# Eight plain gate tiles in the first feed-forward, later sums of the norm, and the low parts of the embedding's gate weights by adding transfers

## The chip, the cores and the metric

The kernel runs on one core of one Trainium2 chip. The metric is device time in microseconds (us) of one execution of the whole program, lower is better; times of several executions are given as their median.

## The reference, cut to what matters

Two layers on 512 tokens of 1024 features, in f32. Each layer adds to `x`: half a gated feed-forward, a token mixer, another half feed-forward, and a gated per-layer embedding; every one of these begins with a norm of `x`.

```
def swiglu_ffn(h, w_gu, w_down):
    a, b = jnp.split(h @ w_gu, 2, axis=-1)
    return (jax.nn.silu(a) * b) @ w_down
...
    for i in range(DEPTH):
        x = x + 0.5 * swiglu_ffn(rms_norm(x, ffn1_norm[i]), ffn1_w_gu[i], ffn1_w_down[i])
        ...
        x = x + 0.5 * swiglu_ffn(rms_norm(x, ffn2_norm[i]), ffn2_w_gu[i], ffn2_w_down[i])
        gate = jax.nn.sigmoid(rms_norm(x, ple_norm[i]) @ ple_w_gate[i])
        x = x + gate * (p[i] @ ple_w_proj[i])
    return rms_norm(x, final_norm)
```

The feed-forward's inner width is 1408, which is 11 tiles of 128 columns; a "gate tile" is one such tile of the gate half `a` and of the up half `b` together.

## The kernel before, in words

**Layout and precision.** `x` is held as eight tiles `x[m]` of 128 features by 512 tokens. Every product is three matmuls in a reduced f32 format (fp32r): each operand is split into a high part (a rounded copy) and a low part (the value minus the rounded copy), and high·high, high·low and low·high are summed in PSUM. For a weight tile, `w_cut` (L259) does this: ACT copies the high part into `wh` (L260), DVE subtracts it from the loaded tile `wr` to give `wl` (L261). A tile of weights is loaded by one SP transfer (`w_load`), from a ring of `WR` = 8 buffers (5 of them ahead for ungrouped tiles), and `wh` and `wl` have `WS` = 4 buffers each. `weight` (L321) hands out the weights in the order of a `plan` made up front, and loads and splits as far ahead as buffers allow. `source` says where in DRAM a planned tile lies.

**The norm.** Its sums of squares are taken by eight narrow matmuls into a bank `pss` (`columns`, L587); `inv_rms` scales them on DVE (`v`, L600) and takes the power on POOL (`rc`, L602). Until `rc` is there, products run on values without it, and the factor is put on behind them.

**The feed-forward, the seven-product way.** `ffn7` (L686) treats a range of gate and up columns (a "group") as a 2 by 2 block matrix and uses seven block products in the place of eight, in the manner of Strassen: B11, B21, T1, T2, B22, T3, T4. Each product is 24 matmuls, so a group of 384 columns (three gate tiles) has 168 matmuls of 384 columns. The weights of T1 to T4 are differences of loaded blocks, made by DVE (`w_term`, L289), and then split as above; for the first group of a feed-forward, T1's are pinned to the order of the program (`w_pin`). The activations of the products come from `Norm7.steps` (L523): per pair of tiles of `x`, sums and differences of half tiles on DVE (L532, L558 to L560) with their high parts on ACT (L534, L562, L563) and low parts on DVE (L538, L567, L569). The results have tokens on partitions and are turned by PE transposes, four to a gate tile, eight together behind the next group's first product (`turn`, L708).

**The first feed-forward of layer 0** has no earlier work to hide its start, so its first `KC` = 5 gate tiles go the plain way (`start` L640, then `gates` L664): per tile two banks A and B of 24 matmuls of 512 columns, scaled by the norm's row R and gated on DVE and ACT (`gated`, L790 to L794, and L401 for the low part). At the end of tile f = 3, `gates` runs `norm.steps` of all eight tiles of `x`. The other six tiles are two groups of 384 columns (`groups_of`, L1657). Late constants, which POOL loads (`late_constants`, L368, transfers L376) and the rotary tables, follow as `during` of the same function.

**Sums in `ffn7`.** In the other three feed-forwards the sums are not yet there when the first group begins, and `norm.sums()` stands behind the product T1 (L744), ahead of the copies of T1's banks (`copies`, L719) and of product T2.

**The embedding's gate of layer 0** (`ple`, L805): eight weight tiles `pg` of 512 KB, each with 24 matmuls into a bank G, and two tiles `pp` for the embedding's own projection J. Behind each G a chain updates a tile of `x`: DVE times R, ACT sigmoid, DVE times J, DVE add, then `steps` of the next norm. From the second tile on DVE is kept in program order here (`Queue`, whose instructions the profile shows as L123). Layer 1's feed-forward, the seven-product way, follows directly.

**Order.** Apart from what is pinned, a planner orders each engine's queue when the kernel is built, by its own cost model; buffers come from pools, 64 slabs of 128 by 512 for the activations.

Of the kernel before, what the change touches and what calls it, by code (L numbers as in the profile page):

```python
# [13 lines left out]
AF = mybir.ActivationFunctionType  # L14
ALU = mybir.AluOpType
# [3 lines left out]
P = 128  # L19
# [3 lines left out]
KD = D // P  # L23
FF = 1408
# [84 lines left out]
def tile_kernel(ctx: ExitStack, tc: tile.TileContext, a: dict, out: bass.AP):  # L109
    nc = tc.nc  # L110
    act, dve, pe, pool = nc.scalar, nc.vector, nc.tensor, nc.gpsimd
# [40 lines left out]
    plan = []  # L152

    def ffn_plan(w, l):
        if (w, l) == (1, 0):
            for f in range(KC):
                plan.append(("gu", f))
                plan.append(("gu", KC + f))
        for g in range(len(groups_of(w, l))):
# [63 lines left out]
    raw, ready = {}, {}  # L223
    at = [0, 0, 0]
    FIRST = 2
# [3 lines left out]
    loads, needs, done = [], [], []  # L229
    base, grouped = {}, set()  # L230
    for key in plan:
# [7 lines left out]
        if g not in base:  # L239
# [3 lines left out]
            n = 2 * groups_of(w_, l_)[g_][1]  # L243
            src = a[f"sg{w_}{l_}{g_}"]
# [18 lines left out]
    def w_tiles():  # L263
        hi = wp.tile([P, WCOLS], F32R, tag="wh", name=nm("wh"), bufs=WS)
        lo = wp.tile([P, WCOLS], F32R, tag="wl", name=nm("wl"), bufs=WS)
        return hi, lo

    def kept(i):

        k = plan[i]  # L270
        return k[0] == "pgl" or (k[0] in ("eo", "oo") and k[1] < OPEN)

    def wc(w, o):
        return w[o // S][:, o % S : o % S + P] if isinstance(w, list) else w[:, o : o + P]

    def w_pin(key):


        if key[3] == 0 and key[4] == "T1":
            return tc.keep_in_program_order  # L280
        return lambda ins: ins
# [18 lines left out]
    def w_split():  # L300
        i = at[1]
        if plan[i][0] == "sg":
            t, n = w_term(plan[i])
            ready[i] = w_tiles()
            w_cut(t, n, *ready[i], slice(0, n), w_pin(plan[i]))
            at[1] += 1
            return
        t, n = raw.pop(needs[i] - 1)
        if kept(i):
            parts = [[sl("kh", F32R) for _ in range(2)], [sl("kl", F32R) for _ in range(2)]]  # L310
            for c in range(2):
                src = t[:, c * S : c * S + S]
                act.copy(parts[0][c], src)
                dve.tensor_tensor(parts[1][c], src, f32(parts[0][c]), op=ALU.subtract)
            ready[i] = parts
        else:
            ready[i] = w_tiles()
            w_cut(t, n, *ready[i], slice(0, n))
        at[1] += 1
# [320 lines left out]
    def start(norm):  # L640

        table("silu_and_others")
        warm = bank("warm")
        for _ in range(WARM):
            pe.matmul(warm, ones_r, ones_r[:, 0:1].to_broadcast([P, S]), start=True, stop=True)
# [18 lines left out]
    def gates(norm, begun):  # L664

        g, wait = [], [begun]
        for f in range(1, KC):
            w = weight("gu", f)
            if f == 1:
                norm.squares()  # L670
            A = proj(w, 0, KD, norm.parts, "A")
            if f == 2:
                norm.sums()
            B = proj(weight("gu", KC + f), 0, KD, norm.parts, "B")
            if f == 2:
                norm.row()
            wait.append((A, B))
            while norm.R is not None and wait:
                gated(*wait.pop(0), norm.R, g)
            if f == 3:  # L680
                for m in range(KD):
                    for _ in norm.steps(m, False):
                        pass
        return g

    def ffn7(w, l, norm, nxt, g=None, during=None, after=None):  # L686


        rc = norm.rc if g else None
        groups = groups_of(w, l)  # L690
        g, turning = g or [], []

        def product(accs, gi, term, first, last):
            n = groups[gi][1]
            units = [weight("sg", w, l, gi, term, u) for u in range(2)]
            for t in range(2):
                for j in range(KD // 2):
                    (h, lw), c = norm.side(term, j)
                    cs = slice(c + t * P, c + t * P + P)
                    wh, wl = units[j // 2]  # L700
                    ws = slice((j % 2) * n, (j % 2) * n + n)
                    o = accs[t][:, :n]
                    begin, end = first and j == 0, last and j == KD // 2 - 1
                    pe.matmul(o, h[:, cs], wh[:, ws], start=begin, stop=False, skip_group_check=True)  # L704
                    pe.matmul(o, h[:, cs], wl[:, ws], start=False, stop=False, skip_group_check=True)  # L705
                    pe.matmul(o, lw[:, cs], wh[:, ws], start=False, stop=end, skip_group_check=True)  # L706

        def turn(count):  # L708
            for _ in range(min(count, len(turning))):
                tiles, i = turning.pop(0)  # L710
                pt = bank("gT")
                for b in range(NB):
                    pe.transpose(pt[:, b * P : b * P + P], tiles[b][:, i * P : i * P + P], ident)
                g.append(split(pt, "g"))

        def copies(accs, n):
            out_ = [sl("r") for _ in range(2)]
            for t in range(2):
                act.copy(out_[t][:, :n], accs[t][:, :n])  # L719
            return out_  # L720

        def add(tiles, accs, n):
            for t in range(2):
                dve.tensor_tensor(tiles[t][:, :n], accs[t][:, :n], tiles[t][:, :n], op=ALU.add)

        def close(c, o, srcs, b0, n):
            for t in range(2):
                r = rc[:, b0 + t : b0 + t + 1]
                act.activation(c[t][:, :n], srcs[t][:, :n], AF.Silu, scale=r)
                dve.scalar_tensor_tensor(o[t][:, :n], o[t][:, :n], r, c[t][:, :n], op0=ALU.mult, op1=ALU.mult)  # L730

        for gi, (_, n) in enumerate(groups):
            two = lambda name: [bank(name) for _ in range(2)]
            al = two("al")
            product(al, gi, "B11", True, False)
            c11 = copies(al, n)
            turn(2)
            be = two("be")
            product(be, gi, "B21", True, True)
            add(c11, be, n)  # L740
            turn(2)
            ga = two("ga")
            product(ga, gi, "T1", True, False)
            if rc is None:  # L744
                rc = norm.sums()
            c22 = copies(ga, n)
            product(al, gi, "T2", False, False)
            c12 = copies(al, n)
            product(ga, gi, "B22", False, True)
            add(c12, ga, n)  # L750
            close(c11, c12, c11, 0, n)
            product(al, gi, "T3", False, False)
            add(c22, al, n)
            product(al, gi, "T4", False, True)
            s2 = [sl("r") for _ in range(2)]
            close(s2, c22, al, 2, n)
            turning.extend(([*c12, *c22], i) for i in range(n // P))
        if during:
            during()

        def part(acc, wt, k0, k1, c0):
            wh, wl = wt
            for kk in range(k0, k1):
                o = slice((kk - c0) * P, (kk - c0) * P + P)
                mm3(acc, wh[:, o], wl[:, o], g[kk][0], g[kk][1], kk == 0, kk == KF - 1)

        cut = DN[0] // P
        early = KF - groups[-1][1] // P
        accs = [bank("dn"), None]
        part(accs[0], weight("dn", w, l, 0, 0), 0, cut, 0)  # L770
        w01 = weight("dn", w, l, 0, 1)
        part(accs[0], w01, cut, early, cut)
        turn(2)
        accs[1] = bank("dn")
        part(accs[1], weight("dn", w, l, 1, 0), 0, cut, 0)
        turn(2)
        part(accs[0], w01, early, KF, cut)
        for m in range(KD):
            if m > 1:
                accs.append(bank("dn"))  # L780
                part(accs[m], weight("dn", w, l, m, 0), 0, cut, 0)
            if m > 0:
                part(accs[m], weight("dn", w, l, m, 1), cut, KF, cut)
            residual(m, accs[m], 0.5, nxt)
            if after and m in after:
                after[m]()
# [870 lines left out]
def groups_of(w, l):  # L1657

    if (w, l) == (1, 0):
        return [(KC * P, 384), (KC * P + 384, 384)]  # L1660
    return [(0, 512), (512, 512), (1024, 384)]


# [4 lines left out]
FREED = {"T3": 2, "T4": 2}  # L1668


KC = 5

EV = (0, 2, 4, 6, 1, 3, 5, 7)
OPEN = 3
WARM = 8
AHEAD = 5
BURST = {"eo": 2, "oo": 1, "pgl": 1}
# [8 lines left out]
def _layout(i):  # L1686
# [7 lines left out]
    gu = i["ffn1_w_gu"][0]  # L1694
    o["gu"] = _tiles(cat([gu[:, : KC * P], gu[:, FF : FF + KC * P]], 1))

# [58 lines left out]
```

## Time and profile before

| what | time |
|---|---|
| median of three runs | 1315.87 us |
| lowest and highest | 1314.79 and 1316.13 us |
| the profiled execution's own time | 1318.16 us |
| its span in the profile | 1316.4 us |

The span runs from the first to the last instruction in the trace. All the other times, of instructions, waits and stretches, are of the one profiled execution, counted from the span's start. A row of a timeline has an instruction's start, its duration, engine, line, operation and tiles, and in brackets the time that its engine was idle before it, with what ended that. PE is the matmul engine, PEld its weight loads; matmuls are pipelined, so that one lasts longer than the distance to the next. PEclk is the granted clock of TensorE, 1.00 being the upper of its two levels, 2.4 GHz, and 0.50 the lower, 1.2 GHz.

### The profile page before, as it was taken

The numbers are of one execution on the slowest core, as the hardware profiler recorded it, in microseconds if no ns is written. First come the engines' busy times: TensorE is split into PE (matmuls) and PEld (weight loads), VectorE is DVE, ScalarE is ACT, GpSimd is POOL, SyncE is SP. The second block draws the span as 40 slices with busy tenths as digits, with TensorE's granted clock in tenths as the row PEclk, the third lists the DMA queues.
The fourth block names the chain that finished last, engine by engine and source line by source line (L and its number), as shares of the span: only waits on it lengthen the run. The fifth ranks groups of instructions, "written<-read, shape, count | busy, mean of one in ns | idle before, by whom it ended". The sixth has DMA issues, their size and how long they took to land.

```text
span 1316.4 us, 16266 instructions
## 1 busy us (share of the span) xinstructions
PE 1280.7 (97%) x6212; PEld 1092.2 (83%) x6212; DVE 910.8 (69%) x1316; ACT 665.1 (51%) x1064; POOL 116.9 (9%) x132
## 2 busy tenths in 40 slices
PE   9969999998999999999989999999999999999997
PEld 7869888886888888988868898888888887898886
DVE  6688763579775998654799875445767598885544
ACT  6455352432654565542655553334778556554442
POOL 0001000425350000000000000000111000000000
PEclk9979999999899999999989999999999999999999
DMA  7023343111300032533203343322113003224401
GB/s 290 34 88 117 109 147 106 45 64 41 121 17 17 0 128 97 160 128 111 81 1 128 97 129 111 128 97 96 65 59 102 16 16 128 93 85 142 145 1 64
DMA packets 39454, 118.66 MB, mean 90 GB/s; under 512 B 4615, under 2 KB 5768, under 8 KB 39376
## 3 DMA queue, kind: packets, MB, share of 16 engines
q1 hardware_dynamic: 38016, 114.64, 26.2%
q0 software_dynamic: 640, 1.89, 0.5%
q8 instruction: 49, 0.80, 0.2%
q10 hardware_dynamic: 720, 1.09, 0.2%
q14 instruction: 29, 0.24, 0.1%
HBM read 115.50 MB, written 2.10 MB: 89 GB/s over the span
## 4 chain that ended last, share of the span: by engine, by line
PE 87%; DVE 9%; ACT 2%; issue 1%; SPq 0%; DMA 0%; POOL 0%; POOLq 0%; DVEq 0%; ACTq 0%
PE dn L395 6%; PE dn L394 6%; PE dn L393 6%; PE al L704 5%; PE al L705 5%; PE al L706 5%; PE ga L705 3%; PE ga L704 3%; PE ga L706 3%; PE sqk L393 2%; PE sqk L395 2%; PE sqk L394 2%; PE val L1016 2%; PE val L1018 2%; PE val L1017 2%; DVE wl L261 1%
## 5 line engine op out<-in xcount | busy, mean ns | idle before, releaser
L260 ACT CAST wh<-wr 128x1024 fp32r<-128x1024 f32 (+3 forms) x299 | 275.4, 925 | 362.2 <-PE dn L394 81.5
L261 DVE TENSOR_TENSOR wl<-wr,wh 128x1024 fp32r<-128x1024 f32 (+3 forms) x292 | 312.7, 1075 | 168.1 <-ACT wh L260 167.4
L395 PE MATMUL dn<-gh,wl 128*128 128x512 f32 x352 | 137.4, 390 | 0.3 <-DVE wl L261 0.2
L393 PE MATMUL dn<-gh,wh 128*128 128x512 f32 x352 | 137.0, 392 | 0.7 <-ACT wh L260 0.7
L394 PE MATMUL dn<-gl,wh 128*128 128x512 f32 x352 | 137.2, 390 | 0.0
L289 DVE TENSOR_TENSOR wr<-wr,wr 128x1024 f32<-128x1024 f32 (+1 forms) x88 | 94.9, 1097 | 0.2
L395 PEld LDWEIGHTS dn<-gh,wl 128*128 128x128 f32 x352 | 66.1, 188 | 14.9 <-DVE wl L261 1.2
L393 PEld LDWEIGHTS dn<-gh,wh 128*128 128x128 f32 x352 | 66.0, 188 | 14.5 <-ACT wh L260 1.1
L394 PEld LDWEIGHTS dn<-gl,wh 128*128 128x128 f32 x352 | 66.1, 188 | 13.8 <-DVE gl L401 0.6
L602 POOL TENSOR_TENSOR rc<-v,half 128x4 f32<-128x4 f32 x8 | 11.8, 1480 | 683.5 <-DVE v L600 683.5
L704 PE MATMUL al<-wh,nvh 128*128 128x512 f32 (+1 forms) x176 | 64.6, 367 | 4.7 <-ACT nvh L534 4.7
L705 PE MATMUL al<-wl,nvh 128*128 128x512 f32 (+1 forms) x176 | 64.5, 366 | 0.0
L706 PE MATMUL al<-wh,nvl 128*128 128x512 f32 (+1 forms) x176 | 64.3, 367 | 0.0
L637 DVE SCALAR_TENSOR_TENSOR x<-dn,x 128x512 f32<-128x512 f32 x32 | 22.1, 691 | 40.9 <-PE dn L395 40.9
L393 PE MATMUL sqk<-xnh,wh 128*128 128x512 f32 x128 | 50.2, 393 | 0.0
L395 PE MATMUL sqk<-xnh,wl 128*128 128x512 f32 x128 | 50.0, 390 | 0.0
L394 PE MATMUL sqk<-xnl,wh 128*128 128x512 f32 x128 | 49.9, 390 | 0.0
L704 PE MATMUL ga<-wh,nuh 128*128 128x512 f32 (+1 forms) x88 | 34.6, 406 | 6.3 <-ACT wh L260 6.3
L704 PEld LDWEIGHTS al<-wh,nvh 128*128 128x128 f32 x176 | 33.2, 189 | 8.9 <-ACT nvh L534 5.1
L481 ACT ACTIVATE sq<-x 128x512 f32<-128x512 f32 x64 | 39.2, 622 | 0.0
L1016 PE MATMUL val<-wh,xnh 128*128 128x512 f32 x96 | 37.5, 391 | 0.0
L1018 PE MATMUL val<-wh,xnl 128*128 128x512 f32 x96 | 37.4, 389 | 0.0
(462 smaller groups left out, 3293.6 us busy)
## 6 DMA issues: line engine op xcount, KB each, us to landing
wr<-in_sg SPq DMA_DIRECT2D x48, 512.0 KB, 4.0
wr<-in_sg SPq DMA_DIRECT2D x40, 384.0 KB, 3.3
wr<-in_dn SPq DMA_DIRECT2D x32, 384.0 KB, 3.1
wr<-in_dn SPq DMA_DIRECT2D x32, 320.0 KB, 3.5
wr<-in_od_qk SPq DMA_DIRECT2D x16, 512.0 KB, 3.2
wr<-in_ev_in SPq DMA_DIRECT2D x12, 512.0 KB, 3.5
wr<-in_gu SPq DMA_DIRECT2D x8, 512.0 KB, 7.2
wr<-in_ev_out SPq DMA_DIRECT2D x8, 512.0 KB, 3.2
```

What stands on the lines that cost most here:

```text
L260: pin(act.copy(hi[:, cs], t[:, cs]))
L261: pin(dve.tensor_tensor(lo[:, cs], t[:, cs], f32(hi)[:, cs], op=ALU.subtract))
L289: sub = lambda o, x, y: pin(dve.tensor_tensor(o[:, :n], x[:, :n], y[:, :n], op=ALU.subtract))
L393: pe.matmul(acc, wh, xh, start=start, stop=False, **k)
L394: pe.matmul(acc, wh, xl, start=False, stop=False, **k)
L395: pe.matmul(acc, wl, xh, start=False, stop=stop, **k)
L481: ins = act.activation(sq, x[m], AF.Square)
L704: pe.matmul(o, h[:, cs], wh[:, ws], start=begin, stop=False, skip_group_check=True)
L705: pe.matmul(o, h[:, cs], wl[:, ws], start=False, stop=False, skip_group_check=True)
L706: pe.matmul(o, lw[:, cs], wh[:, ws], start=False, stop=end, skip_group_check=True)
L1016: pe.matmul(accs[b], xn[k][0][:, bs], wh[:, ws], start=k == 0, stop=False)
L1018: pe.matmul(accs[b], xn[k][1][:, bs], wh[:, ws], start=False, stop=k == KD - 1)
```

## The change

Four edits. `KC` goes from 5 to 8, and the first feed-forward of layer 0 then has a single group of 384 columns. The `steps` of the eight tiles of `x`, which ran together behind tile f = 3, run in pairs behind tiles 3, 4, 5 and 6. In `ffn7`, `norm.sums()` goes from behind product T1 to behind product T2. And the weights `pg` of the embedding's gate get their low part in another way (`w_cut_dma`): ACT copies the high part as before, ACT then writes its negative into `lo`, and a transfer on POOL's queue adds the weight tile from DRAM onto it, so that DVE has no part in it.

```
+    def w_cut_dma(t, src, n, hi, lo):
+        act.copy(hi[:, :n], t[:, :n])
+        act.activation(lo[:, :n], f32(hi)[:, :n], AF.Copy, scale=-1.0)
+        pool.dma_start(lo[:, :n], src, accum_op=ALU.add)
...
+        elif plan[i][0] in BY_DMA and needs[i] > FIRST:
+            ready[i] = w_tiles()
+            w_cut_dma(t, loads[needs[i] - 1][0], n, *ready[i])
         else:
             ready[i] = w_tiles()
             w_cut(t, n, *ready[i], slice(0, n))
...
-            if f == 3:
-                for m in range(KD):
+            if f >= 3 and f < 3 + KD // 2:
+                for m in (2 * f - 6, 2 * f - 5):
                     for _ in norm.steps(m, False):
                         pass
...
+            c22 = copies(ga, n)
+            product(al, gi, "T2", False, False)
             if rc is None:
                 rc = norm.sums()
-            c22 = copies(ga, n)
-            product(al, gi, "T2", False, False)
             c12 = copies(al, n)
...
     if (w, l) == (1, 0):
-        return [(KC * P, 384), (KC * P + 384, 384)]
+        return [(KC * P, FF - KC * P)]
...
-KC = 5
+KC = 8
...
+BY_DMA = ("pg",)
```

## Rows read from the trace of the kernel before

**Rows 1.** The page: busy time of the engines, granted TensorE clock by slice.
```profile
PE 1280.7 (97%) x6212; PEld 1092.2 (83%) x6212; DVE 910.8 (69%) x1316; ACT 665.1 (51%) x1064; POOL 116.9 (9%) x132
...
PEclk9979999999899999999989999999999999999999
```

**Rows 2.** The waits, engine PE, whole span: total us, times, longest us.
```profile
PE ga L704 <- ACT wh L260: 6.3, 2, 5.1
PE al L704 <- ACT nvh L534: 4.7, 1, 4.7
PE pss L587 <- DVE sqa L489: 3.3, 1, 3.3
PE pss L587 <- DVE sqa L123: 2.0, 1, 2.0
```

**Rows 3.** Windows: us; busy PE, PEld, DVE, ACT, POOL; PEclk, DMA share, GB/s.
```profile
52.45:63.33 10.88, 10.88 (x49) 9.01 (x48) 8.86 (x15) 6.43 (x13) 0.00 (x0) 1.00 0.00 1
63.33:107.37 44.04, 34.13 (x170) 32.08 (x169) 37.53 (x57) 22.70 (x38) 8.13 (x11) 0.84 0.33 102
107.37:137.85 30.48, 30.48 (x181) 30.42 (x181) 25.19 (x34) 17.80 (x27) 0.00 (x0) 1.00 0.36 112
77.90:91.50 13.60, 8.43 (x23) 7.02 (x24) 12.31 (x18) 8.34 (x15) 2.84 (x5) 0.50 0.32 94
654.60:693.00 38.40, 34.69 (x133) 27.26 (x133) 36.61 (x54) 21.11 (x32) 1.92 (x1) 0.87 0.00 1
```

**Rows 4.** Timeline of PE in both groups of the first feed-forward.
```profile
77.93 0.64 PE L704 MATMUL al<-wh,nvh 128*128 128x384 f32 x1 [4.75 <-ACT nvh L534]
...
85.36 1.01 PE L704 MATMUL ga<-wh,nuh 128*128 128x384 f32 x2 [5.06 <-ACT wh L260]
...
111.53 1.04 PE L713 MATMUL gT<-ident,r 128*128 128x128 f32 x8
```

**Rows 5.** Groups of DVE instructions, shapes apart, 52.45 to 107.37 us.
```profile
L261 DVE TENSOR_TENSOR wl<-wr,wh 128x768 fp32r<-128x768 f32 x15 | 14.7, 993 | 5.5 <-ACT wh L260 5.5
L289 DVE TENSOR_TENSOR wr<-wr,wr 128x768 f32<-128x768 f32 x10 | 9.5, 949 | 0.0
L567 DVE TENSOR_TENSOR nul<-nu,nuh 128x512 fp32r<-128x512 f32 x4 | 2.8, 688 | 0.3 <-ACT nuh L562 0.3
...
L560 DVE SCALAR_TENSOR_TENSOR nw<-x,gains,nu 128x256 f32<-128x256 f32 x4 | 1.9, 481 | 0.1
...
L532 DVE TENSOR_TENSOR nv<-nv,ne 128x256 f32<-128x256 f32 x4 | 1.7, 421 | 0.2
```

**Rows 6.** Timelines of PE, ACT, DVE at sums in layer 1's first feed-forward.
```profile
685.42 1.75 PE L587 MATMUL pss<-ones,sqa 128*128 128x2 f32 x8 [1.98 <-DVE sqa L123]
...
685.12 2.00 ACT L260 CAST wh<-wr 128x1024 fp32r<-128x1024 f32 x2
...
687.21 0.16 DVE L600 TENSOR_SCALAR v<-pss 128x4 f32<-128x4 f32 x1 [0.65 <-PE pss L587]
```

**Rows 7.** Timelines of ACT and PE in the embedding gate, DVE behind it.
```profile
602.42 1.06 ACT L260 CAST wh<-wr 128x1024 fp32r<-128x1024 f32 x1 [2.35 <-PE dn L394]
...
627.13 1.05 ACT L260 CAST wh<-wr 128x1024 fp32r<-128x1024 f32 x1 [0.26 <-PE J L394]
...
613.06 0.39 PE L395 MATMUL G<-xnh,wl 128*128 128x512 f32 x1
...
641.72 0.39 PE L395 MATMUL G<-xnh,wl 128*128 128x512 f32 x1
...
654.57 1.23 DVE L123 TENSOR_TENSOR wl<-wr,wh 128x1024 fp32r<-128x1024 f32 x1 [0.57 <-ACT wh L260]
```

**Rows 8.** DMA view (KB each, median us to landing); one POOL issue (timeline).
```profile
wr<-in_pg SPq DMA_DIRECT2D x8, 512.0 KB, 3.2
...
craw<-in_consts POOLq DMA_DIRECT2D x3, 256.0 KB, 3.1
...
82.66 0.54 POOL L376 DMA_DIRECT2D craw<-in_consts  x1 [0.59 <-DVE bb L793]
```

## The prediction, made before the changed kernel was run

> **What bounds the kernel now.** I began with the page. PE is busy 97% of the span [rows 1], so a time can only come down where PE does less work, stands idle, or runs at the lower clock. The granted clock has its one deep dip, 7 tenths, in the third slice, 66 to 99 us at 33 us a slice: the first feed-forward. So the next view was the waits of PE. Three of its largest waits lie where the change works: 6.3 us for a high part of weights, 4.7 us for a high part of the norm's tiles, and 3.3 and 2.0 us for the squares behind the sums [rows 2]. The windows then price the stages. A plain tile takes 10.88 us with PE busy throughout; the first group of 384 columns takes 44.04 us, the second, with the same arithmetic and 12 transposes more, 30.48 us [rows 3]. The timeline shows why: waits of 4.75 us at 77.93 and 5.06 us at 85.36 [rows 4], and between 77.90 and 91.50 us a granted clock of 0.50, the lower level, which followed PE's first long idle time [rows 3]. In that stretch DVE is busy 12.31 of 13.60 us: DVE is late there, and what makes it late is the steps of all eight tiles of `x` at one point, among the first group's subtractions and cuts.
>
> **Part 1, eight plain tiles.** Removed: both groups, 44.04 + 30.48 = 74.52 us. Added: three plain tiles, 3 x 10.88 = 32.64 us [rows 3], and one group. An undisturbed product is 24 matmuls, from 107.37 us, where the second group's window begins, to the turning at 111.53 [rows 3, 4]: 4.16 us, so a group of seven is 29.12 us. After: 61.76 us, a gain of 12.76 us, which I take as 12.8. Three plain tiles cost 3.5 us more than an undisturbed group would; the gain is all in that the disturbed group goes. The lower bound for a group that runs clean is the whole second group with its turning, 30.48 us: a gain of 11.4.
>
> Does DVE keep up? Steps per pair of tiles: two low parts at 0.69, two scaled operations at 0.48 and three differences at 0.42 [rows 5], 3.6 us. Gating is four operations of 512 columns, taken at 0.69 like the low part in rows 5: 2.8 us. Two cuts of 1024 columns at 1.23 [rows 7]: 2.5 us. Together 8.9 us of a tile's 10.88; the tile of 52.45 us already had 8.86 us of DVE work with PE never waiting [rows 3]. The steps are over one tile before the group begins. In the group, ahead of T1 stand the last gating 2.8, two cuts of B21 at 0.99, two subtractions at 0.95 and two cuts of T1 at 0.99 [rows 5]: 8.7 us, against 8.3 us until T1 starts and 1 us more until its second unit is used (six matmuls of 4.16 / 24). Cuts run up to four tiles ahead, so B21's begin before the group. I take no wait; the margin is small, and it returns as a rival.
>
> **Part 2, the sums behind T2.** In layer 1's first feed-forward the sums wait 1.98 us for the last sum of squares, but ACT begins the next weights' two high parts only at 685.12, and the first ends about 1 us later; PE had the sums done by about 687.1 [rows 6]. Without the sums it would wait for the weights until about 686.2: 0.9 us at most, taken as 0.6. The other place (3.3 us, layer 1's second feed-forward) has the same order of things; I take 0.2. Bounds for both: 5.3 us gained if the waits simply go [rows 2], nothing if the planner leaves them in place. A later factor delays the first silu by one product; DVE's `v` and POOL's power, under 2 us [rows 3], lie under product B22, 24 matmuls that follow, so I cost that at nothing. Sums moved 0.8 us in all.
>
> **Part 3, the adding transfers.** Removed: eight DVE cuts of 1.23 us [rows 7]. In the gate itself DVE is not what PE waits for; behind it, from 654.60 to 693.00, DVE is busy 36.61 of 38.40 us and the clock is 0.87 [rows 3], so earlier DVE time would be worth something there. But at 654.57 DVE had been idle 0.57 us for a cut by ACT [rows 7]: it had caught up, all eight cuts of `pg` lay before that, and the crowded stretch begins no earlier without them. Gain taken: 0. Upper bound: PE's idle time there, 38.40 - 34.69 = 3.7 us, and for the clock some as much.
>
> Added: eight ACT passes of about 1.06 us, on an engine that is busy 51% of the span [rows 1], and eight issues by POOL of 0.54 us [rows 8]. What counts is how long the low part takes: high part 1.06, negative 1.06, issue 0.54, then the landing. No row shows an adding transfer. The nearest are the plain load of the same tile by SP, 3.2 us for 512 KB, and a POOL transfer of 256 KB, 3.1 us [rows 8], twice which is 6.2. I take 6.2, as an add must also read what it adds to: 8.9 us in all. The room is, for the first tile, from the high part at 602.42 to the first matmul with the low part at 613.06, 10.6 us, and for the fifth from 627.13 to 641.72, 14.6 us [rows 7]. So no wait. POOL's power for the gate's own norm stands in the same queue, behind an issue that itself waits for ACT's two passes, 1.06 + 1.06 + 0.54 = 2.7 us at most; its result scales the G banks on DVE, which PE doesn't wait for while banks are free, so I count nothing, and if banks run out up to those 2.7 us.
>
> Here the Trainium skill speaks against the change. The POOL transfers of the constants landed in 3.1 us while DVE was busy 12.31 of 13.60 us [rows 3, 8], so busy DVE work of that mix did not starve them. SBUF — State Buffer, section "A bandwidth-pool intuition that's wrong (but worth ruling out)", says that a transfer issued by POOL can wait for descriptors while DVE copies, about 620 ns becoming about 3100 ns. By that rule the landing would be five times the plain 3.2 us, about 16 us, an estimate from that page, and the time about 1319 by the price of the third rival below; by the row the sum stays. No run here shows an adding transfer beside DVE's work in the gate.
>
> **Sum.** -12.8 - 0.8 + 0 = -13.6 us: the profiled execution's 1318.16 becomes 1304.6. It stands 2.29 us above the median 1315.87, to which the same gain applies: **1302.3 us**. A difference of 0.2%, 2.6 us, is about what a measurement of this kernel can tell from none.
>
> **The rivals.** *Relief is worth something:* DVE, free of `pg`, does more steps before 654 us, and the waits and the lower clock behind are cut by 2 to 4 us: 1298.3 to 1300.3. Against it stands the idle 0.57 us at 654.57. Chance 0.10.
>
> *The stall comes back in the one group:* T1's pinned work, 8.7 us in 9.4, comes late behind the last gating, one of the two waits of rows 4 remains, and with it half of the first group's excess of 44.04 - 30.48 = 13.56 us: 6.8 us, 1309.1. For it: the thin margin, and a planner that may put the gating ahead. Chance 0.08.
>
> *The adding transfers land late (slower).* If high part to landed low part takes L, the first tile waits L - 10.6 and, as its buffers come free so much later but its followers shift too, the fifth waits L - 14.6 anew [rows 7]. The first group lost 13.56 us by waits of 9.81 us, 1.38 us for one of waiting, the clock included [rows 3, 4]. The whole gain is gone when 1.38 x (2L - 25.2) = 13.6, at L = 17.5, a landing of 14.9 us. From 15.8 us on the kernel is slower by over 0.2%; at 18 us of landing, L = 20.7, waits of 16.2 cost 22.3: 1324.6. Against it: 3.1 and 3.2 us in rows 8, a fifth of that. For it: no accumulating transfer is seen, and POOL's queue carried little. Chance 0.12 for landings over 14 us, 0.08 of it slower and 0.04 within 0.2%.
>
> *Partly late:* landings of 9 to 14 us make L 11.7 to 16.7; the first tile waits 1.1 to 6.1 and the fifth up to 2.1, 1.5 to 11.3 us: 1303.8 to 1313.6. Chance 0.12, of which 0.02 within 0.2%.
>
> **How the numbers follow.** The forecast case has 0.58 and its own range of 1300 to 1305, from the bounds of the group (11.4) and of the sums (a few us more if both waits go). With relief, stall and partly late landings the range is 1298.5 to 1311, leaving out the late transfers, the top of the partly late ones and the ends: under 2 in 10. Faster by over 0.2%: 0.58 + 0.10 + 0.08 + 0.10 = 0.86; within: 0.02 + 0.04 = 0.06; slower: 0.08.
>
> **What would show it.** Right: plain tiles f = 5 to 7 at 10.9 us each with no wait of PE, one group of about 29 us at clock 1.00, no 4.7 and 5.1 us waits in the list, and a time 12 to 13 us less from 63 us to the down projection. The sums' waits of 2.0 and 3.3 us gone, and in layer 1 under 1 us less from T1 to B22. Landings of the adding transfers under 9 us, and no PE wait in the gate. Wrong: a wait of G's matmuls for a low part with a clock under 1.00 between 605 and 650 us; or a wait at T1 in the one group.

## The result and the profile after

| | before | after |
|---|---|---|
| median of four runs | 1315.92 us | 1302.01 us |
| lowest and highest | 1314.79 and 1316.13 us | 1301.33 and 1303.54 us |
| the profiled execution's time | 1318.16 us | 1301.74 us |
| its span | 1316.4 us | 1300.0 us |

The ratio is 0.9898, with an interval from 0.988 to 0.9915: 13.9 us less by the medians, somewhere from 11 to 16. The forecast was 1302.3, in a range of 1298.5 to 1311. The total was right, but not every term of it. The inserted lines move the line numbers: L587 of the kernel before is L597 in the changed kernel, and L602 in the runs with three more tiles.

The page of the changed kernel, engines and granted clock by slice:

```profile
PE 1274.2 (98%) x6176; PEld 1082.2 (83%) x6176; DVE 890.5 (69%) x1291; ACT 665.1 (51%) x1057; POOL 122.9 (9%) x140
...
PEclk9999999999999999999989999999999999999999
```

PE is busy for 6.5 us less than in [rows 1], and the dip of the clock to 7 tenths in the third slice is gone. (It isn't less matmul work: three plain tiles have more of it than the group that they replace. Less of it runs at the lower clock.) The waits of PE (total us, times, longest us):

```profile
PE pss L597 <- DVE sqa L123: 3.6, 1, 3.6
PE pss L597 <- DVE sqa L499: 3.3, 1, 3.3
...
PE al L715 <- DVE wl L261: 0.4, 1, 0.4
...
PE ga L714 <- ACT wh L260: 0.3, 1, 0.3
```

Of the four lines of [rows 2] the 4.7 us are gone and nearly all of the 6.3. (The 6.3 are two waits: 5.06 us in the first feed-forward, which is gone, and 1.28 us in layer 1's first, which is now 0.3.) The two for the sums are still there, one as long as before and one longer (3.6 for 2.0). The windows, with the columns of [rows 3]; the sixth plain tile (f = 5), the last, the one group, and the crowded stretch behind the embedding's gate:

```profile
62.80:73.70 10.90, 10.90 (x49) 9.02 (x49) 9.18 (x16) 5.91 (x12) 0.00 (x0) 1.00 0.23 72
84.60:95.48 10.88, 10.88 (x49) 9.01 (x48) 7.64 (x13) 5.39 (x11) 2.93 (x6) 1.00 0.21 71
95.48:125.43 29.95, 29.58 (x169) 29.06 (x168) 25.84 (x33) 16.02 (x24) 4.14 (x6) 1.00 0.44 133
638.00:676.40 38.40, 34.10 (x138) 26.75 (x137) 37.03 (x55) 22.14 (x33) 1.95 (x1) 0.91 0.00 1
```

A plain tile takes 10.9 us, PE without a pause, and DVE is busy 7.6 to 9.2 us of it; the group takes 29.95 us at full clock. Three tiles and the group are 62.6 us for the 74.52 of [rows 3]: **11.9 us less**. The last row is the stretch that had 0.87 in [rows 3], 16.6 us earlier, which is within 0.9 us of the same work: DVE is no less busy than it was, 37.03 us for 36.61.

The rest of the 16.4 us between the two profiled spans was found by matching where the same products begin in both traces: 0.5 us ahead of the first feed-forward's row R, where the two kernels still run the same work; 3.4 us in layer 0's token mixer, which the change doesn't touch; 1.0 us in the crowded stretch, where the embedding's gate passes into layer 1's first feed-forward; and 0.2 us given back in layer 1's second feed-forward. The first question was whether the 3.4 us are the change's.

### The profile page after: what moved, and what is told of

Read it like the earlier page. It is cut to its first block, busy times and chain, and to the rows that moved or that the text cites. A ratio compares the mean times of both kernels' runs of the same rounds, so it can differ in the third digit from the quotient of the medians.

```text
span 1300.0 us, 16177 instructions
## 1 busy us (share of the span) xinstructions
PE 1274.2 (98%) x6176; PEld 1082.2 (83%) x6176; DVE 890.5 (69%) x1291; ACT 665.1 (51%) x1057; POOL 122.9 (9%) x140
## 4 chain that ended last, share of the span: by engine, by line
PE 87%; DVE 9%; ACT 1%; issue 1%; DMA 0%; POOL 0%; SPq 0%; POOLq 0%; DVEq 0%; ACTq 0%
PE dn L405 6%; PE dn L404 6%; PE dn L403 6%; PE al L714 5%; PE al L715 5%; PE al L716 5%; PE ga L715 2%; PE ga L716 2%; PE ga L714 2%; PE sqk L403 2%; PE sqk L405 2%; PE sqk L404 2%; PE val L1026 2%; PE val L1028 2%; PE val L1027 2%; DVE wl L261 1%
## 5 line engine op out<-in xcount | busy, mean ns | idle before, releaser
L260 ACT CAST wh<-wr 128x1024 fp32r<-128x1024 f32 (+3 forms) x283 | 261.4, 928 | 335.7 <-PE dn L404 78.9
L261 DVE TENSOR_TENSOR wl<-wr,wh 128x1024 fp32r<-128x1024 f32 (+3 forms) x280 | 301.0, 1079 | 162.5 <-ACT wh L260 161.8
L296 DVE TENSOR_TENSOR wr<-wr,wr 128x1024 f32<-128x1024 f32 (+1 forms) x80 | 87.1, 1111 | 0.1
L716 PE MATMUL al<-wh,nvl 128*128 128x512 f32 (+1 forms) x160 | 58.8, 367 | 0.0
L612 POOL TENSOR_TENSOR rc<-v,half 128x4 f32<-128x4 f32 x8 | 11.9, 1488 | 495.6 <-DVE v L610 495.6
L714 PE MATMUL al<-wh,nvh 128*128 128x512 f32 (+1 forms) x160 | 58.8, 367 | 0.0
L715 PE MATMUL al<-wl,nvh 128*128 128x512 f32 (+1 forms) x160 | 58.8, 367 | 0.0
L1027 PE MATMUL val<-wl,xnh 128*128 128x512 f32 x96 | 37.4, 390 | 0.0
L418 DVE SCALAR_TENSOR_TENSOR xnl<-x,gains,xnh 128x512 fp32r<-128x512 f32 x40 | 29.9, 750 | 8.8 <-ACT xnh L416 7.7
```

The source lines that it names most:

```text
L260: pin(act.copy(hi[:, cs], t[:, cs]))
L261: pin(dve.tensor_tensor(lo[:, cs], t[:, cs], f32(hi)[:, cs], op=ALU.subtract))
L296: sub = lambda o, x, y: pin(dve.tensor_tensor(o[:, :n], x[:, :n], y[:, :n], op=ALU.subtract))
L1027: pe.matmul(accs[b], xn[k][0][:, bs], wl[:, ws], start=False, stop=False)
```

## The experiments

**The kernel before, unaltered, profiled again.**

> The kernel before, unchanged, for a second profile. In the profiled executions 3.35 us of the difference lie in the token mixer of layer 0, which the change doesn't touch and where every engine has the same order of work in both kernels. If that is what one execution differs from another by, this profile's span is 1313 to 1316 us and its mixer does not have the dip of the clock to 0.80 of the first profile; if the mixer is slower in this kernel for a reason, it is there again and the span is 1316 us.

Its time was 1315.29 us, its span 1313.5. In the mixer every engine of both kernels has the same order of work. The first fence is two windows of the first profile of before, the second the wait of PE ahead of them in the new one (it was 2.00 us at 326.05 in the first, too), the third the new one's windows:

```profile
330.00:335.00 5.00, 5.00 (x19) 4.46 (x19) 3.79 (x10) 3.51 (x7) 0.53 (x1) 0.50 0.79 249
335.00:340.00 5.00, 5.00 (x30) 4.43 (x29) 2.07 (x4) 3.48 (x5) 0.00 (x0) 0.76 0.46 172
```

```profile
326.55 3.16 PE L1273 MATMUL pa<-mq,mk 128*128 128x128 f32 x16 [2.00 <-DVE mq L1264]
```

```profile
330.00:335.00 5.00, 5.00 (x29) 4.50 (x29) 4.29 (x12) 3.86 (x7) 0.53 (x1) 0.88 0.83 252
335.00:340.00 5.00, 5.00 (x39) 4.69 (x38) 4.10 (x8) 4.92 (x8) 0.00 (x0) 1.00 0.74 237
```

The same wait of 2.00 us, in the same kernel, was followed by 10 us at 0.50 and 0.76 of the clock in one execution, and by 0.88 and 1.00 in the other. By matched products the mixer of one and the same kernel took 2.5 us more in the first execution, and the mixer's 3.4 us are mostly that, not the change: against the second profile its part of the difference is 0.8 us. The other two places vary as well. The two profiles of the kernel before differ by 0.4 us ahead of row R and by 0.8 us in the crowded stretch, and against the second of them the changed kernel gains 0.2 us in that stretch. The feed-forward's gain alone is the same against both, 11.9 and 12.0 us. On the chip of these runs the kernel before had a median of 1314.47 us in 23 runs, from 1312.85 to 1319.18.

**The parts alone.** The tiles, the one group and the steps in pairs:

```
-KC = 5
+KC = 8
...
-        return [(KC * P, 384), (KC * P + 384, 384)]
+        return [(KC * P, FF - KC * P)]
...
-            if f == 3:
-                for m in range(KD):
+            if f >= 3 and f < 3 + KD // 2:
+                for m in (2 * f - 6, 2 * f - 5):
```

> Eight plain tiles, one group and the steps in pairs, without the other two edits. My theory: this is nearly the whole gain, 11.5 to 13 us, so 1303 to 1304.5. If the transfers relieve DVE by as much as the median suggests beyond that, the time is 1305 or more.

1302.4 us, ratio 0.9912 (0.9894 to 0.993). The full change had 0.9898 (0.988 to 0.9915); the intervals overlap, so the tiles are the gain, as far as these runs can tell. (It is 0.6 us under the range that I had expected.)

The adding transfers alone, with the function `w_cut_dma` as in the change:

```
...
+        elif plan[i][0] in BY_DMA and needs[i] > FIRST:
+            ready[i] = w_tiles()
+            w_cut_dma(t, loads[needs[i] - 1][0], n, *ready[i])
...
+BY_DMA = ("pg",)
```

> Adding transfers alone, on the kernel before. My theory: no gain by DVE's relief, and about 1 us by the order of ACT's queue behind the gate, so 1315 to 1316. The rival, that DVE's relief is worth 2 to 4 us: 1312 to 1314. The other rival, a late landing: over 1317.

1315.54 us in twelve runs, ratio 1.0002 (0.999 to 1.0015): no difference that these can show. Its waits, and the landing of its transfers (KB each, median us from issue to landing):

```profile
PE ga L714 <- ACT wh L260: 5.4, 2, 5.1
PE al L714 <- ACT nvh L544: 4.7, 1, 4.7
PE pss L597 <- DVE sqa L123: 3.6, 1, 3.6
```

```profile
wl<-in_pg POOLq DMA_DIRECT2D x8, 512.0 KB, 7.2
```

Here the first feed-forward's stall is that of before, and the wait for the sums behind the gate is 3.6 us, as in the changed kernel: that is the transfers' doing. ACT's queue behind the gate was reordered, the wait for a weight's high part ahead of the sums fell from 1.28 to 0.31 us, PE came to the sums earlier, and waited for the late DVE there.

The sums behind T2 alone:

```
             ga = two("ga")
             product(ga, gi, "T1", True, False)
-            if rc is None:
-                rc = norm.sums()
             c22 = copies(ga, n)
             product(al, gi, "T2", False, False)
+            if rc is None:
+                rc = norm.sums()
```

> The sums behind product T2 alone. The planner leaves the sums where they were in both feed-forwards of layer 1, among product T1, and moves them only in the second feed-forward of layer 0, where PE did not wait. So my term of 0.8 us should be 0: 1315.5 to 1316.3, and the waits of 2.0 and 3.3 us are still there. If the place of the sums mattered: 1313 to 1315.

1315.23 us, ratio 1.0008 (0.9996 to 1.0021). The waits for the sums are those of [rows 2], to a tenth:

```profile
PE pss L587 <- DVE sqa L489: 3.3, 1, 3.3
PE pss L587 <- DVE sqa L123: 2.0, 1, 2.0
```

The edit moves the sums in the program's text, but the planner orders PE's queue, and puts them among T1's matmuls again. In the changed kernel the timeline of PE shows them there; `ga` belongs to T1 and `al` to T2:

```profile
668.61 1.25 PE L597 MATMUL pss<-ones,sqa 128*128 128x2 f32 x8 [3.60 <-DVE sqa L123]
669.72 1.20 PE L714 MATMUL ga<-wh,nuh 128*128 128x512 f32 x2
670.72 0.63 PE L714 MATMUL al<-wh,nuh 128*128 128x512 f32 x1
```

**What in the first feed-forward does it?** The changed kernel, with all steps at one point again:

```
-            if f >= 3 and f < 3 + KD // 2:
-                for m in (2 * f - 6, 2 * f - 5):
+            if f == 3:
+                for m in range(KD):
```

> The changed kernel with the steps of all eight tiles of x back behind tile f = 3, before four more plain tiles. If the gain comes from putting plain tiles, with some 5 us of free DVE time each, behind the steps, the 14 us of DVE work drain before the group begins, and the time is that of the changed kernel within 1 us. If the spreading itself is needed, PE waits for cuts in tiles 4 and 5 and the lower clock follows: 5 us or more over the changed kernel, 1307 or more.

1303.64 us, ratio 0.9917 (0.9904 to 0.993), 1.6 us over the changed kernel's median where I had expected 1 us at most. In its profile that time isn't in the feed-forward: it is lost at about 247 us, where the mixer begins, and the profile with three more tiles below loses it there, too. In the first feed-forward the spreading isn't needed: the windows of the tiles f = 5 and 6 show the same 10.90 us, with DVE at 8.9 to 9.3 us in each.

```profile
62.80:73.70 10.90, 10.90 (x50) 9.03 (x49) 8.93 (x16) 6.51 (x12) 0.00 (x0) 1.00 0.14 43
73.70:84.60 10.90, 10.90 (x50) 9.03 (x49) 9.32 (x17) 5.77 (x11) 0.00 (x0) 1.00 0.25 74
```

The steps run wherever DVE has time, for four plain tiles behind them ask little of it. The other way round, five plain tiles and both groups, with the steps spread:

```
-KC = 8
+KC = 5
...
-        return [(KC * P, FF - KC * P)]
+        return [(KC * P, 384), (KC * P + 384, 384)]
...
-            if f >= 3 and f < 3 + KD // 2:
-                for m in (2 * f - 6, 2 * f - 5):
+            if f >= 1 and f < 1 + KD // 2:
+                for m in (2 * f - 2, 2 * f - 1):
```

> The changed kernel with five plain tiles and two groups as before, but the steps in pairs behind tiles 1 to 4. My account says that three plain tiles cost 3.5 us more than an undisturbed group, so with both groups clean this takes 59.6 us for what takes 61.8: 1300. DVE has three gatings behind tile 2, though, about 14.5 us of work in 10.9, so a rest of some 4 us may reach the first group: then 1301 to 1306. If plain tiles are needed for another reason (the pinned work of T1 is late whenever a group begins so early), the stall of the kernel before is back: 1308 or more.

1307.83 us, ratio 0.9961 (0.9947 to 0.9975). That lies between what I had expected (1306 at most) and the rival (1308 or more), next to the rival. The two waits of [rows 4] are shorter, 3.56 and 1.97 us for 4.75 and 5.06, but there; the last row is the window ahead of the first of them:

```profile
76.49 0.45 PE L714 MATMUL al<-wh,nvh 128*128 128x384 f32 x1 [3.56 <-ACT nvh L544]
...
80.62 1.01 PE L714 MATMUL ga<-wh,nuh 128*128 128x384 f32 x2 [1.97 <-ACT wh L260]
...
68.00:76.00 8.00, 4.93 (x29) 4.61 (x27) 8.00 (x14) 3.13 (x7) 0.00 (x0) 1.00 0.00 0
```

DVE is busy for all 8.00 us there, and the last pair's steps, in the program behind tile 4, come in the middle of the group's work: DVE begins them at 75.36 us. So starting the steps two tiles earlier takes back part of the stall; with more plain tiles, spread or not, nearly all of it goes. What counts is DVE's room, not the steps' place in the program.

Seven plain tiles and a group of 512 columns:

```
-KC = 8
+KC = 7
```

> The changed kernel with seven plain tiles and one group of 512 columns. By the sum, one plain tile of 10.88 us less and a group of 168 matmuls at 0.227 us, 38.1 us, for one at 0.173, 29.1: 1.9 us less, so 1300. The rival, that the steps' last pair is now right ahead of the group and T1 comes late: a wait of 2 to 5 us and the lower clock, 1304 to 1309.

1304.46 us, ratio 0.9926 (0.9915 to 0.9938), 2.5 us over the changed kernel's first median where I had expected 1.9 under it, and at the low edge of the rival. Gates, group and all take as long as with eight, so the 1.9 us of the sum are spent on small waits, 0.9 us for the norm's last high part and 0.7 us for T1's second low part, the two that the rival had in mind. Here no plain tile stands between the last steps and the group, and the stall is this small all the same. The down projection behind takes 4 us longer, with a wait for the last turned gate tile and a clock of 0.93 in the window from 140 to 165 us:

```profile
PE dn L403 <- ACT gh L409: 1.2, 1, 1.2
PE al L714 <- ACT nvh L544: 0.9, 1, 0.9
```

```profile
140.00:165.00 25.00, 22.53 (x88) 17.05 (x87) 19.25 (x30) 13.29 (x21) 0.00 (x0) 0.93 0.28 89
```

**Transfers where DVE is the bound.** To the changed kernel, three more tiles by adding transfers: those of B11 and B21 in layer 1's first feed-forward, inside the stretch where DVE is busy 37.03 of 38.40 us.

```
-            w_cut(t, n, *ready[i], slice(0, n), w_pin(plan[i]))
+            if plan[i][1:] in SG_DMA:
+                _, w_, l_, g_, term, u_ = plan[i]
+                b = ("B11", "B21").index(term)
+                w_cut_dma(t, loads[base[plan[i][:4]] + 2 * b + u_][0], n, *ready[i])
+            else:
+                w_cut(t, n, *ready[i], slice(0, n), w_pin(plan[i]))
...
+SG_DMA = ((1, 1, 0, "B11", 0), (1, 1, 0, "B11", 1), (1, 1, 0, "B21", 0))
```

> The changed kernel, with the low parts of three more weight tiles by adding transfers: both units of B11 and the first of B21 in the first group of layer 1's first feed-forward, where DVE is busy 37.0 of 38.4 us and PE waits 3.6 us for the last sum of squares at the lower clock. Three cuts of 1.23 us less on DVE there: if DVE is the bound, the sums come 3 us or more earlier and 3 to 5 us go, 1297 to 1299. If a landing of 6.8 us makes B11's second unit or B21's first late, or ACT's extra passes delay the steps, nothing is gained or 1 to 5 us are lost.

1299.41 us, ratio 0.9887 (0.9874 to 0.9901). PE's waits, then two windows: the same 38.40 us of the crowded stretch, and from B11's first matmul to the second group's first turning.

```profile
PE pss L602 <- DVE sqa L504: 3.3, 1, 3.3
PE pss L602 <- DVE sqa L123: 1.9, 1, 1.9
```

```profile
640.36:678.76 38.40, 36.38 (x161) 28.97 (x160) 36.98 (x55) 28.02 (x40) 4.55 (x4) 1.00 0.31 58
652.34:699.88 47.54, 45.52 (x202) 36.47 (x201) 45.93 (x56) 28.01 (x36) 1.96 (x1) 1.00 0.29 98
```

The wait for the sums fell to 1.9 us, the two small ones ahead of it are gone, and the clock stays at 1.00. In the changed kernel the second of these windows is this:

```profile
649.98:702.94 52.96, 48.66 (x202) 38.72 (x200) 49.27 (x60) 29.06 (x38) 1.95 (x1) 0.94 0.25 80
```

5.4 us in the profiles, 2.6 in the medians, though these are not of runs side by side. To have them side by side, the changed kernel was run once more on one chip with the three that follow.

> The changed kernel, unaltered, beside the next three on one chip. Ratio to the kernel before 0.989 to 0.991, as measured first.

1301.8 us (1300.34 to 1302.22), ratio 0.9901 (0.9881 to 0.9922) to a median of 1313.52 of the kernel before beside it. The same window:

```profile
650.77:702.18 51.41, 47.11 (x202) 37.40 (x200) 49.12 (x60) 28.96 (x38) 1.95 (x1) 0.97 0.24 83
```

And with the three tiles as above, but without the embedding's eight:

```
-BY_DMA = ("pg",)
+BY_DMA = ()
+SG_DMA = ((1, 1, 0, "B11", 0), (1, 1, 0, "B11", 1), (1, 1, 0, "B21", 0))
```

> The kernel with three tiles of B11 and B21 by adding transfers, but the embedding's eight gate tiles by DVE again. My theory: the transfers of the gate tiles are worth nothing, because DVE waits for PE's gate banks there, and those of B11 and B21 are worth 3 to 5 us because DVE is the bound behind them. So this is as fast as with both: 3 us or more under the changed kernel. If the eight and the three only work together (DVE must also be ahead when the stretch begins), this is within 1.5 us of the changed kernel.

1299.55 us (1299.17 to 1301.17), ratio 0.9889 (0.9867 to 0.9911); four of its five times lie under all six of the changed kernel's beside it. That is 2.3 us less, short of the 3 I had written, and as fast as with all eleven tiles.

```profile
PE pss L602 <- DVE sqa L123: 2.7, 1, 2.7
```

```profile
650.23:701.07 50.84, 48.10 (x202) 39.09 (x201) 46.42 (x56) 28.77 (x37) 1.95 (x1) 0.93 0.28 90
```

By the medians it is as fast as the one with eleven, with less in it, and faster than the changed kernel by an amount near what these runs resolve. The profile shows only part of that where the three tiles act: the window is 0.6 us shorter than the one beside it (2.1 us than the first), and 1.5 us more are gained in layer 1's second feed-forward, which this edit leaves alone. With all eleven tiles the window was 47.54 us, 3.3 us less than here. So whether the eight add something to the three is open: the medians, of two chips, differ by 0.1 us, and one profile of each can't decide it.

Then, to this, two tiles more in layer 1's second feed-forward, where the other wait for the sums is:

```
-SG_DMA = ((1, 1, 0, "B11", 0), (1, 1, 0, "B11", 1), (1, 1, 0, "B21", 0))
+SG_DMA = ((1, 1, 0, "B11", 0), (1, 1, 0, "B11", 1), (1, 1, 0, "B21", 0), (2, 1, 0, "B11", 1), (2, 1, 0, "B21", 0))
```

> The same, and two tiles more by adding transfers in layer 1's second feed-forward (second unit of B11, first of B21), where PE waits 3.3 us for the last sum of squares behind a DVE that is busy 46.5 of 50 us. Two cuts less, 2.4 us: if DVE is the bound there too, the wait falls to about 1 us and 2 to 4 us go with the lower clock behind it. The first unit of B21 has 9.8 us from its high part to its use, about what a transfer takes, so a late landing may take the gain back: then no difference to the kernel without them.

1302.04 us, ratio 0.9906 (0.9884 to 0.9928): the gain of the three is gone.

```profile
PE pss L602 <- DVE sqa L504: 4.2, 1, 4.2
...
PE be L721 <- DVE nol L571: 0.4, 1, 0.4
```

The wait for the sums grew from 3.3 to 4.2 us, and the stretch of that feed-forward from B11's first matmul to the second group's first turning from 49.8 us to 52.7, the clock's part included. No PE wait for a late transfer is in the list, so it was not the landing; ACT's two more passes and a new order of the queues may have delayed the steps, but which of them did it was not tried.

**The price of a late transfer.** To the changed kernel: the first gate tile in two transfers, the second behind the first. Both add the weights to minus twice the high part, so that this tile's low part comes out doubled; that is what the kernel computes differently.

```
-        act.activation(lo[:, :n], f32(hi)[:, :n], AF.Copy, scale=-1.0)
-        pool.dma_start(lo[:, :n], src, accum_op=ALU.add)
+        act.activation(lo[:, :n], f32(hi)[:, :n], AF.Copy, scale=-float(times))
+        for _ in range(times):
+            pool.dma_start(lo[:, :n], src, accum_op=ALU.add)
...
+            w_cut_dma(t, loads[needs[i] - 1][0], n, *ready[i], times=2 if plan[i][-1] == 0 else 1)
```

> The changed kernel with the first gate tile added in two transfers, one behind the other, onto minus twice the high part, so that its low part lands some 7 us later (and is twice the low part, which is the part of the computation that differs). It had 0.9 us to spare, so PE waits about 6.5 us there once. By the price of my slower rival, 1.38 us for one of waiting, the time is 9 us over the changed kernel; without the lower clock behind the wait, 6.5 us; if the gate's chain behind it has slack that takes it up, under 3 us.

1310.77 us (twelve runs, 1308.05 to 1314.7), 9.0 us over the changed kernel beside it. From the timelines, PE's wait and the first issue; then the window of the 15 us about it:

```profile
600.81 0.79 PE L406 MATMUL G<-xnh,wl 128*128 128x512 f32 x1 [4.60 <-DMA wl<-in_pg]
...
588.34 0.94 POOL L282 DMA_DIRECT2D wl<-in_pg  x1 [141.51 <-ACT wl L280]
```

```profile
597.00:612.00 15.00, 11.19 (x41) 9.11 (x42) 1.16 (x5) 2.11 (x2) 1.95 (x2) 0.77 0.64 129
```

The second transfer landed at 600.8, and PE waited 4.60 us, not 6.5: the two together took 12.5 us from the first issue at 588.34, about twice this profile's median landing of 6.1 us, and 6.8 was the changed kernel's. In this profile the gate took 7.6 us longer (60.8 us from its first matmul to the feed-forward's, for 53.1): 1.66 us for one of waiting, with the clock at 0.77 in the window.

## Why the prediction was right, and where it was not

**Part 1 (12.8 us) held, and is the whole gain.** The stretch gave 11.9 us: tiles 10.9, as taken from the row, and a group of 29.95 us where seven undisturbed products made 29.12. That is the mis-sized term. From one product's first matmul to the next one's, five of the seven take 4.16 to 4.19 us, as priced; T1 takes 4.32 and T2 4.80, and each of these two lost its time at its second low part:

```profile
109.89 0.45 PE L715 MATMUL al<-wl,nuh 128*128 128x384 f32 x1 [0.37 <-DVE wl L261]
```

This is T2. At T1, the place where the prediction had weighed 8.7 us against 9.4, DVE came in time to within 0.2 us: "I take no wait; the margin is small" was right there. The wait came one product later, where the prediction had not looked: DVE has no pause between T1's cuts and T2's. Both effects together are 0.8 us, and with them the gain from 63 us to the down projection is just under the 12 to 13 us that the prediction had named as a sign.

Of what made DVE late, the prediction named two things together, the steps "at one point" and their place "among the first group's subtractions and cuts". The runs leave the second. With all the steps at one point, but four plain tiles behind them, there is no stall (10.90 us a tile, 1303.64), and five plain tiles with spread steps keep much of it (1307.83): the room behind the steps is the cure.

**Part 2 (0.8 us) failed.** The step was "taken as 0.6" and "I take 0.2", where the text had named the lower bound itself: nothing, if the planner leaves the sums in place. It did in both places that had a wait. In the one place where it moved them (layer 0's second feed-forward) nothing waited. The true term is 0, ratio 1.0008 alone, and the sign that the prediction had named, both waits gone, did not show.

**Part 3 (0) held, for the reason given.** Alone the transfers are worth 1.0002. DVE's first cut behind the gate starts at 638.80 us, 15.77 us earlier than the 654.57 of [rows 7], which is by how much everything before it is earlier; DVE had been idle 2.57 us for ACT there, for 0.57. The relief turned into idle time ahead of the crowded stretch, as the prediction said. The chain of the first tile in the changed kernel, ACT's two passes, POOL's issue and the matmul that wants the result, with DVE's cut behind the gate as the last row; and the landings:

```profile
586.66 1.06 ACT L279 CAST wh<-wr 128x1024 fp32r<-128x1024 f32 x1 [2.35 <-PE dn L404]
...
588.24 1.04 ACT L280 ACTIVATE wl<-wh 128x1024 fp32r<-128x1024 f32 x1
...
589.59 0.94 POOL L281 DMA_DIRECT2D wl<-in_pg  x1 [141.53 <-ACT wl L280]
...
597.29 0.39 PE L405 MATMUL G<-xnh,wl 128*128 128x512 f32 x1
...
638.80 1.23 DVE L123 TENSOR_TENSOR wl<-wr,wh 128x1024 fp32r<-128x1024 f32 x1 [2.57 <-ACT wh L260]
```

```profile
wr<-in_pg SPq DMA_DIRECT2D x8, 512.0 KB, 3.2
wl<-in_pg POOLq DMA_DIRECT2D x8, 512.0 KB, 6.8
```

The landing was sized well: 6.8 us, estimated as 6.2 from twice the POOL row of 256 KB. The issue took 0.94, for 0.54. From ACT's start at 586.66 to an assumed landing at 589.59 + 6.8 = 596.4 are 9.7 us of a room of 10.6. So 0.9 us was to spare, which is thin.

The prediction had set against this sum a landing of about 16 us. The case that the Trainium skill gives (SBUF — State Buffer, section "A bandwidth-pool intuition that's wrong (but worth ruling out)") is a transfer that waits for descriptors while DVE runs a `tensor_copy`; to make five times the plain landing of it, for other DVE work, was the prediction's own scaling, an estimate. The landings of 6.1 to 7.2 us don't bear it out, but in the gate DVE was no hard test: freed of the eight cuts, it is busy 23.00 us of 52.14. The harder test is the run with three more tiles, where DVE is busy 11.15 of the 12.50 us in which they were in flight, and they landed sooner:

```profile
586.66:638.80 52.14, 52.14 (x235) 43.26 (x234) 23.00 (x38) 33.55 (x46) 8.09 (x9) 1.00 0.76 181
...
642.90:655.40 12.50, 12.50 (x57) 10.36 (x56) 11.15 (x21) 9.88 (x15) 2.60 (x3) 1.00 0.78 128
...
wl<-in_sg POOLq DMA_DIRECT2D x3, 512.0 KB, 5.6
```

That work is operations on two tensors; a DVE that copies was not tried.

**The rivals.** The slower one's mechanism is real and its point of decision plausible, though it did not occur: made late by a second transfer, one wait of 4.6 us cost 7.6 us in the profile and 9.0 by the medians, 1.7 to 2 us for one of waiting, more than the 1.38 that it was priced with. The stall in the one group came back as 0.4 us only. Relief behind the gate was there to be had, but not from these eight tiles alone: with three others, 2.3 us by the medians.

The total came out to 0.3 us of the forecast partly by luck: 0.9 us too much for the group and 0.8 for the sums were made up by time that no term stands for. In the profiles it lies in the mixer and about the gate, where executions of one kernel differ. In the medians it lies with the kernel before: the four runs beside the changed kernel had 1315.92, and the three later sets, of 12 to 23 runs, 1313.52 to 1314.47, while the changed kernel hardly moved, 1302.01 and 1301.8. In that second set it was 11.7 us under the kernel before, which is closer to what the terms add up to, 11.9 + 0 + 0.

## What to carry to other kernels

When an engine is late at one place, price the change by what stands between its work and the deadline: here four plain tiles, each with some us of free DVE time, did what spreading the work in the program did not. Before moving an instruction in the text, see whether the text decides its place; where a planner does, compare the queues. And take work off an engine where it has no idle time left until PE next waits for it: eight cuts ahead of an idle gap bought nothing by themselves, three behind it some 2 us. That is no rule to go by unmeasured: two more in a place that looked the same lost those 2 us again.

## What the runs showed of the hardware

An accumulating transfer of 512 KB on POOL's queue landed in 6.1 to 7.2 us (medians of the runs with the embedding's eight tiles), about twice the 3.2 us of the plain load of the same tile; those in layer 1's feed-forwards landed in 5.4 to 5.6 us (medians of three runs), against 3.8 to 4.3 us for the plain loads of that size from the same input. POOL took 0.86 to 0.94 us to issue one. And the same wait of PE is not worth the same each time: behind 2.00 us of idle time, with the same order of work, in the 10 us from 330 the clock stood at the lower level for some 7 us in one execution and between 1 and 2 in another (worked out from the means of the windows). Between stalls it can even trade places: in two profiles of the changed kernel the stretch behind the embedding's gate took 52.96 and 51.41 us, and the same stretch of layer 1's second feed-forward, with the same waits, 50.07 and 51.25. A difference of a us or so in one stage of one profile is therefore no gain yet. Side by side, 17 runs of the kernel before scatter over 1311 to 1320 us, and six of the changed kernel, with two of the stalls less, over 1300.3 to 1302.2; that the stalls make the difference is not shown, and twelve runs with one longer stall scatter over 1308 to 1315.
